# Hybrid encoder trunk, last down projection: token slices of 384 and 128 instead of 256 and 256

## The chip, the cores and the metric

The kernel runs on one core of one Trainium2 chip. The metric is the device time of one execution in microseconds, on the slowest core (here the only one). Three timed runs of the kernel before took 1594.29, 1595.68 and 1596.27 us; the median is 1595.68.

## The reference

Two layers work on 512 tokens of width 1024. Each layer projects a normalized input into three mixers (a retention, a diagonal state-space model, a gated linear attention), merges them with gates, and ends with a squared-ReLU MLP. A final norm follows. What matters here is the last part:

```
    for l in range(DEPTH):                     # DEPTH = 2
        ...
        h2 = rmsnorm(x, norm2_g[l])
        x = x + jnp.square(jax.nn.relu(h2 @ w_ff1[l])) @ w_ff2[l]     # 1024 -> 4096 -> 1024
    return rmsnorm(x, final_norm_g)

def rmsnorm(x, g):
    xf = x.astype(jnp.float32)
    y = xf * lax.rsqrt(jnp.mean(xf * xf, axis=-1, keepdims=True) + EPS)
    return (y * g.astype(jnp.float32)).astype(x.dtype)
```

All of it is float32.

## The kernel before

Everything is kept transposed: features on the 128 partitions, tokens along the free axis. `x` is 8 tiles of 128 features by 512 tokens. A weight chunk of 128 × 1024 (`raw`) is loaded by DMA and split into two fp32r parts, a rounded one (`whi`, line 108, ScalarE) and the rest (`wlo`, line 109, VectorE). Activations are split in the same way (`fh` and `fl` for the hidden tiles of the MLP). A product is then three fp32r matmuls per block of 128 features, high by high, high by low, low by high (lines 125 to 127 in `col_tile`), 24 for one output tile of 128 features, all into one PSUM tile `mm`, of which four rotate.

The MLP's 4096 hidden features are worked through in four quarters. A quarter makes 8 hidden tiles and then multiplies them with the matching part of the second weight matrix, for each of the 8 output tiles `j`, and adds to `x[j]`. For the fourth quarter of the last layer (line 442) the loop is turned: all 8 weight chunks are kept (`ws`), and the tokens are cut into two slices. For each slice the 8 output tiles are computed one after the other (24 matmuls each), each is added to `x` on VectorE (line 451), its square is taken on ScalarE and summed over the tiles on GpSimd (`acc_sq`, lines 174 to 178), and the output times the gain is prepared on ScalarE (`scale_out`, line 241). `emit_out` then ends a slice with the final norm:

- column sums over the features by matmuls of the accumulators with a column of ones, one matmul for each 128 tokens and each of two accumulators (line 155, plain f32);
- the mean and its inverse square root in twelve small VectorE operations on one value per token (lines 158 and 134 to 141);
- a diagonal matrix for each 128 tokens (line 162), and a product with ones (line 164) that spreads the values over all partitions, copied to SBUF by ScalarE (line 166);
- eight products of output and norm, six on VectorE (line 253) and two on GpSimd (line 251), and four DMAs, each for a pair of tiles (line 255).

Each engine works through its own instructions in the order in which a scheduler put them at build time, from dependencies and from the priorities that `hp` sets. The first slice's norm is therefore put between the matmuls of the second slice; the second slice's norm has nothing behind it and ends the kernel.

Of the kernel before, what the change touches and what calls it, by code (L numbers as in the profile page):

```python
# [17 lines left out]
P = 128  # L18
# [21 lines left out]
class Hybrid:  # L40
# [264 lines left out]
    def layer(self, l, h, acc):  # L305
# [69 lines left out]
        for j2 in range(4):  # L375
            w = self.weights(l)
            for i in range(2):
                j = 2 * j2 + i
                ps = self.col_tile(w, yc, base=i * 512)
# [3 lines left out]
        for j4 in range(2):  # L383
            w = self.weights(l)
            for i in range(4):
                j = 4 * j4 + i
                ps = self.col_tile(w, ya, base=i * 256)
# [5 lines left out]
        for j2 in range(4):  # L393
            gb = [gate(8 + 2 * j2 + i) for i in range(2)]
            w = self.weights(l)
            for i in range(2):
                j = 2 * j2 + i
# [12 lines left out]
        for j in range(KT):  # L410
# [4 lines left out]
            ps = self.col_tile(w, ms)  # L415
# [12 lines left out]
        for q in range(4):  # L428
            hid = []
            for f in range(8):  # L430
                w = self.weights(l)
                ps = self.col_tile(w, h2)
                with self.hp(15000):
                    t = self.slot(s="ht")
                    ev = nc.vector.scalar_tensor_tensor(t, ps, 0.0, R2, ALU.max, ALU.mult)  # L435
                    nc.scalar.square(t, t)  # L436
                    hi, lo = self.slot(F32R, s="fh"), self.slot(F32R, s="fl")
                    self.split(hi, lo, t)
                    hid.append((hi, lo))
                if q and f < 6:  # L440
                    self.bg_steps(1, ev)
            if q == 3 and l + 1 == self.depth:
                ws = [self.weights(l, "wt") for _ in range(KT)]
                for sl in (slice(0, 256), slice(256, 512)):
                    acts = [(a[:, sl], b[:, sl]) for a, b in hid]
                    acc, out = [], []
                    for j in range(KT):
                        ps = self.col_tile(ws[j], acts, ps=self.mm([P, 256]))
                        with self.hp(15000):
                            xj = self.x[j][:, sl]  # L450
                            nc.vector.tensor_add(xj, xj, ps)
                            self.acc_sq(acc, xj, j)
                            out.append(self.scale_out(j, sl))
                    with self.hp(15000):
                        self.emit_out(acc, out, sl)
                break
            for j in range(KT):
                w = self.weights(l)
                ps = self.col_tile(w, hid)
                with self.hp(15000):  # L460
                    ev = nc.vector.tensor_add(self.x[j], self.x[j], ps)  # L461
                    if q == 3:
                        xs = self.dr.tile([P, 512], F32, tag=f"xs{j}", bufs=1, name=self.nm("xs"))
                        nc.sync.dma_start(xs, self.x[j])
                        self.xsrc[j] = xs
                        hn.append(self.scaled_split(self.x[j], self.smc(l + 1, SM_G1, j)))
                        self.acc_sq(acc, self.x[j], j, two=False)
                if q < 3 and j < 7:
                    self.bg_steps(2, ev)
# [720 lines left out]
```

## Time and profile before

| | |
|---|---|
| median of three runs | 1595.68 us |
| profiled execution, its own time | 1598.12 us |
| its span, first to last instruction | 1596.2 us |
| TensorE busy in the span | 1567.2 us (98%), 7862 matmul records |
| VectorE, ScalarE, GpSimd busy | 957.3 (60%), 589.4 (37%), 176.1 (11%) us |
| mean granted TensorE clock | 0.988 |
| share of TensorE in the chain that ended last | 87% |

The profiled execution is 2.44 us above the median. Its span leaves out 1.92 us of that execution. PE stands for TensorE's matmuls and PEld for its weight loads, which run beside them; DVE is VectorE, ACT is ScalarE, POOL is GpSimd. A matmul's record is longer than the distance to the next one, since matmuls are pipelined: how often they come is read from starts, not from durations.

### The profile page before, as it was taken

What the parts mean: (1) busy time and instruction counts of PE and PEld (TensorE: products, weight loads), DVE (VectorE), ACT (ScalarE), POOL (GpSimd) and SP (SyncE); (2) the same over time, 40 slices, a digit from 0 to 9 for tenths busy, and PEclk for the clock granted to TensorE, in tenths of its full rate; (3) what the DMA queues carried; (4) which work ended last, traced back from release to release, by engine and by line L of the source; (5) the groups of instructions that cost most, each with busy time, mean ns of one, the idle gap of its engine ahead of it and who ended that gap; (6) DMA issues with size and microseconds to landing.
All of it is one profiled execution on the core that took longest, in us unless ns stands there. A gap on an engine that the chain in (4) does not pass through costs nothing.

```text
span 1596.2 us, 20251 instructions
## 1 busy us (share of the span) xinstructions
PE 1567.2 (98%) x7862; PEld 1320.0 (83%) x7862; DVE 957.3 (60%) x1678; ACT 589.4 (37%) x917; POOL 176.1 (11%) x212
## 2 busy tenths in 40 slices
PE   9998799999999999999999999999999999999997
PEld 6987788888888887888889898878888888888897
DVE  6798888665645747434557858945556534343353
ACT  5543153424434243423425333242334423232242
POOL 0113102331210000000111110210312000000001
PEclk9999799999999999999999999999999999999998
DMA  6522122332432323232335322332334232323221
GB/s 211 167 67 86 60 78 83 107 114 80 150 106 79 107 90 111 80 110 94 128 121 156 93 87 73 106 119 79 102 115 140 93 96 91 105 92 106 92 67 54
DMA packets 60512, 163.35 MB, mean 102 GB/s; under 512 B 10556, under 2 KB 17212, under 8 KB 60416
## 3 DMA queue, kind: packets, MB, share of 16 engines
q1 hardware_dynamic: 60096, 161.01, 31.7%
q8 instruction: 62, 1.02, 0.2%
q0 software_dynamic: 320, 1.05, 0.2%
q14 instruction: 34, 0.28, 0.1%
HBM read 147.11 MB, written 6.52 MB: 96 GB/s over the span
## 4 chain that ended last, share of the span: by engine, by line
PE 87%; DVE 10%; DMA 1%; issue 1%; SPq 0%; POOL 0%; ACT 0%; DVEq 0%; POOLq 0%
PE mm L126 26%; PE mm L127 26%; PE mm L125 26%; DVE wlo L109 1%; PE mm L284 1%; PE mm L286 1%; PE mm L282 1%; PE ms L555 1%; PE ms L1056 1%; DMA rsw<-za 0%; PE ms L1021 0%; DVE mean L642 0%; DMA xp<-xT 0%; PE ms L691 0%; PE ms L155 0%
## 5 line engine op out<-in xcount | busy, mean ns | idle before, releaser
L125 PE MATMUL mm<-hh,whi 128*128 128x512 f32 x1136 | 445.9, 393 | 0.3 <-ACT whi L108 0.3
L127 PE MATMUL mm<-hh,wlo 128*128 128x512 f32 x1136 | 445.4, 393 | 0.6 <-DVE wlo L109 0.6
L126 PE MATMUL mm<-hl,whi 128*128 128x512 f32 x1136 | 445.7, 392 | 0.0
L108 ACT CAST whi<-raw 128x1024 fp32r<-128x1024 f32 (+1 forms) x258 | 266.9, 1043 | 362.4 <-PE mm L127 227.0
L109 DVE TENSOR_TENSOR wlo<-raw,whi 128x1024 fp32r<-128x1024 f32 (+1 forms) x258 | 341.6, 1325 | 87.5 <-PE mm L126 65.6
L125 PEld LDWEIGHTS mm<-hh,whi 128*128 128x128 f32 x1136 | 214.2, 189 | 45.4 <-issue 1.2
L127 PEld LDWEIGHTS mm<-hh,wlo 128*128 128x128 f32 x1136 | 214.0, 188 | 44.8 <-DVE wlo L109 1.3
L126 PEld LDWEIGHTS mm<-hl,whi 128*128 128x128 f32 x1136 | 214.1, 188 | 44.7 <-issue 0.7
L126 PE MATMUL mm<-fl,whi 128*128 128x512 f32 (+1 forms) x576 | 210.9, 366 | 0.0
L127 PE MATMUL mm<-fh,wlo 128*128 128x512 f32 (+1 forms) x576 | 210.5, 366 | 0.0
L125 PE MATMUL mm<-fh,whi 128*128 128x512 f32 (+1 forms) x576 | 209.5, 366 | 0.0
L126 PEld LDWEIGHTS mm<-fl,whi 128*128 128x128 f32 x576 | 108.6, 189 | 17.7
L125 PEld LDWEIGHTS mm<-fh,whi 128*128 128x128 f32 x576 | 108.5, 189 | 17.6
L127 PEld LDWEIGHTS mm<-fh,wlo 128*128 128x128 f32 x576 | 108.6, 189 | 17.5
L178 POOL TENSOR_TENSOR acc<-acc,sq 128x512 f32<-128x512 f32 (+1 forms) x30 | 33.7, 1123 | 683.0 <-ACT sq L177 680.5
L461 DVE TENSOR_TENSOR x<-x,mm 128x512 f32<-128x512 f32 x56 | 38.4, 685 | 113.8 <-PE mm L127 113.8
L436 ACT ACTIVATE ht<-ht 128x512 f32<-128x512 f32 x64 | 40.4, 632 | 152.2 <-DVE ht L435 152.2
L435 DVE SCALAR_TENSOR_TENSOR ht<-mm,R 128x512 f32<-128x512 f32 x64 | 44.1, 689 | 86.4 <-PE mm L127 75.1
L114 DVE TENSOR_TENSOR fl<-ht,fh 128x512 fp32r<-128x512 f32 x64 | 44.2, 691 | 69.1 <-ACT fh L113 69.0
L369 ACT ACTIVATE g<-g,cst 128x512 f32<-128x512 f32 x48 | 34.8, 724 | 114.0 <-DVE g L368 113.8
L126 PE MATMUL mm<-y,whi 128*128 128x512 f32 x160 | 62.2, 389 | 0.0
L127 PE MATMUL mm<-y,wlo 128*128 128x512 f32 x160 | 62.2, 389 | 0.0
(266 smaller groups left out, 2049.6 us busy)
## 6 DMA issues: line engine op xcount, KB each, us to landing
raw<-wst SPq DMA_DIRECT2D x254, 512.0 KB, 3.7
dup<-zc SPq DMA_DIRECT2D x32, 128.0 KB, 3.6
rsw<-za SPq DMA_DIRECT2D x32, 64.0 KB, 2.6
qfb<-za SPq DMA_DIRECT2D x16, 128.0 KB, 4.2
x<-xT SPq DMA_DIRECT2D x8, 256.0 KB, 4.0
xs<-x SPq DMA_DIRECT2D x8, 256.0 KB, 2.9
x<-xs SPq DMA_DIRECT2D x8, 256.0 KB, 4.4
outT<-out SPq DMA_DIRECT2D x8, 256.0 KB, 2.7
```

The source lines that it names most:

```text
L108: nc.scalar.copy(hi[:, s], raw[:, s])
L109: nc.vector.tensor_sub(lo[:, s], raw[:, s], hi[:, s].bitcast(F32))
L114: self.nc.vector.tensor_sub(lo, src, hi.bitcast(F32))
L125: nc.tensor.matmul(ps, hi[:, o:o + P], a, start=first and k == 0, stop=False)
L126: nc.tensor.matmul(ps, hi[:, o:o + P], b, start=False, stop=False)
L127: nc.tensor.matmul(ps, lo[:, o:o + P], a, start=False, stop=last and k == n - 1)
L178: return (eng or (nc.vector if j == KT - 1 else nc.gpsimd)).tensor_add(accs[0], accs[0], t)
L282: nc.tensor.matmul(o, a[:, s], hi[:, k * 256:(k + 1) * 256], start=f, stop=False, skip_group_check=True)
L369: nc.scalar.activation(g, g, AF.Sigmoid, bias=self.smc(l, SM_BM, j))
L435: ev = nc.vector.scalar_tensor_tensor(t, ps, 0.0, R2, ALU.max, ALU.mult)
L436: nc.scalar.square(t, t)
L461: ev = nc.vector.tensor_add(self.x[j], self.x[j], ps)
```

## The change

The two slices of tokens have 384 and 128 tokens instead of 256 and 256, and the PSUM tile takes its width from the slice.

```diff
             if q == 3 and l + 1 == self.depth:
                 ws = [self.weights(l, "wt") for _ in range(KT)]
-                for sl in (slice(0, 256), slice(256, 512)):
+                for sl in (slice(0, 384), slice(384, 512)):
                     acts = [(a[:, sl], b[:, sl]) for a, b in hid]
                     acc, out = [], []
                     for j in range(KT):
-                        ps = self.col_tile(ws[j], acts, ps=self.mm([P, 256]))
+                        ps = self.col_tile(ws[j], acts, ps=self.mm([P, sl.stop - sl.start]))
```

Both kernels have the same number of instructions on each engine. Of column sums and diagonal products the first slice now has three for each accumulator or norm and the second one, instead of two and two.

On TensorE, in the first output tile of the second slice, before (`mm_12543` is its PSUM tile, `acc_12287` an accumulator of the first slice, the last column the output's shape):

```order
L125 MATMUL mm_12543<-fh_12057,whi_12215 128x256
L126 MATMUL mm_12543<-fl_12058,whi_12215 128x256
L127 MATMUL mm_12543<-fh_12057,wlo_12216 128x256
L155 MATMUL ms_12503<-cst,acc_12287 128x1 x2
L125 MATMUL mm_12543<-fh_12095,whi_12215 128x256
L126 MATMUL mm_12543<-fl_12096,whi_12215 128x256
```

The same place after the change, where that tile is `mm_12546`:

```order
L125 MATMUL mm_12546<-fh_12019,whi_12215 128x128
L126 MATMUL mm_12546<-fl_12020,whi_12215 128x128
L127 MATMUL mm_12546<-fh_12019,wlo_12216 128x128
L155 MATMUL ms_12503<-cst,acc_12287 128x1 x3
L125 MATMUL mm_12546<-fh_12057,whi_12215 128x128
L126 MATMUL mm_12546<-fl_12058,whi_12215 128x128
```

The second slice's matmuls have 128 columns, and the first slice's column sums, now three, stand three matmuls earlier in it.

On VectorE, in the middle of the second slice, before (line 451 adds a tile of the second slice, lines 141 and 162 belong to the first slice's norm, line 253 multiplies the first slice's outputs by it):

```order
L141 SCALAR_TENSOR_TENSOR ny_12512<-nu_12514,ny_12512 128x2
L451 TENSOR_TENSOR x_9918<-x_9918,mm_12573 128x256
L162 TENSOR_SCALAR dg_12524<-cst,ny_12512 128x128 x2
L451 TENSOR_TENSOR x_9959<-x_9959,mm_12603 128x256
L253 TENSOR_TENSOR out_12289<-out_12289,ms_12527 128x256 x2
L253 TENSOR_TENSOR out_12350<-out_12350,ms_12527 128x256
L253 TENSOR_TENSOR out_12411<-out_12411,ms_12527 128x256 x2
L253 TENSOR_TENSOR out_12472<-out_12472,ms_12527 128x256
L451 TENSOR_TENSOR x_10000<-x_10000,mm_12634 128x256
```

The same place after the change:

```order
L140 TENSOR_TENSOR nu_12516<-nu_12516,nv_12510 128x3
L451 TENSOR_TENSOR x_9918<-x_9918,mm_12576 128x128
L141 SCALAR_TENSOR_TENSOR ny_12514<-nu_12516,ny_12514 128x3
L162 TENSOR_SCALAR dg_12526<-cst,ny_12514 128x128 x3
L451 TENSOR_TENSOR x_9959<-x_9959,mm_12606 128x128
L253 TENSOR_TENSOR out_12289<-out_12289,ms_12530 128x384 x2
L253 TENSOR_TENSOR out_12350<-out_12350,ms_12530 128x384
L253 TENSOR_TENSOR out_12411<-out_12411,ms_12530 128x384 x2
L253 TENSOR_TENSOR out_12472<-out_12472,ms_12530 128x384
L451 TENSOR_TENSOR x_10000<-x_10000,mm_12637 128x128
```

The second slice's second addition stands one place earlier, there are three diagonal products, and the first slice's products with the norm are 384 columns wide, still ahead of the fourth addition.

## Rows read from the trace of the kernel before

**Rows 1.** Busy time by stretch: us, PE, PEld, DVE, ACT, POOL, clock, DMA.

```profile
1536.60:1560.77 24.17, 24.17 (x202) 24.13 (x202) 5.79 (x11) 7.65 (x18) 4.43 (x6) 1.00 0.00 1
1560.77:1583.85 23.08, 23.08 (x195) 23.02 (x193) 7.28 (x27) 6.14 (x16) 5.82 (x8) 1.00 0.14 47
1583.85:1596.20 12.35, 2.15 (x9) 1.27 (x9) 4.93 (x21) 1.19 (x3) 1.41 (x2) 0.67 0.25 85
```

**Rows 2.** Timeline, VectorE: start, us, line, names, shapes, idle before and releaser.

```profile
1503.84 0.69 DVE L435 SCALAR_TENSOR_TENSOR ht<-mm,R 128x512 f32<-128x512 f32 x1 [1.57 <-PE mm L127]
1509.28 0.69 DVE L435 SCALAR_TENSOR_TENSOR ht<-mm,R 128x512 f32<-128x512 f32 x1 [1.57 <-PE mm L127]
...
1553.78 0.42 DVE L451 TENSOR_TENSOR x<-x,mm 128x256 f32<-128x256 f32 x1 [2.46 <-PE mm L127]
1556.65 0.42 DVE L451 TENSOR_TENSOR x<-x,mm 128x256 f32<-128x256 f32 x1 [2.46 <-PE mm L127]
```

**Rows 3.** Timeline, TensorE: f32 passes of 128 and of 64 moving columns.

```profile
263.25 1.95 PE L1021 MATMUL ms<-U,s5PT 128*128 128x128 f32 x16
264.95 0.48 PE L127 MATMUL mm<-hh,wlo 128*128 128x512 f32 x1
265.27 0.40 PE L125 MATMUL mm<-hh,whi 128*128 128x512 f32 x1
...
962.35 0.39 PE L691 MATMUL ms<-v,rsT 128*128 128x64 f32 x2
962.57 0.39 PE L692 MATMUL ms<-rS,qfb 128*128 128x64 f32 x2
```

**Rows 4.** Weight loads by shape: line, names, shapes, count, busy us, mean ns.

```profile
L125 PEld LDWEIGHTS mm<-fh,whi 128*128 128x128 f32 x576 | 108.5, 189 | 17.6
...
L1021 PEld LDWEIGHTS ms<-U,s5PT 128*128 128x128 f32 x128 | 15.8, 192 | 0.5
```

**Rows 5.** Chain that ended last, in time order: start, us, what.

```profile
1583.88 0.43 DVE x L451
1584.33 0.42 ACT acc L174
...
1584.80 0.62 PE ms L155 x4
...
1587.81 0.49 DVE dg L162 x2
...
1588.35 1.23 PE ms L164 x2
...
1589.60 0.38 ACT R L166
...
1590.01 0.42 DVE out L253
...
1590.76 1.32 DVE out L253 x4
```

**Rows 6.** Groups by shape: count, busy us, mean ns, idle before and releaser.

```profile
L461 DVE TENSOR_TENSOR x<-x,mm 128x512 f32<-128x512 f32 x56 | 38.4, 685 | 113.8 <-PE mm L127 113.8
...
L177 ACT ACTIVATE sq<-x 128x512 f32<-128x512 f32 x21 | 12.9, 616 | 0.0
...
L451 DVE TENSOR_TENSOR x<-x,mm 128x256 f32<-128x256 f32 x16 | 6.6, 420 | 32.4 <-PE mm L127 32.4
...
L177 ACT ACTIVATE sq<-x 128x256 f32<-128x256 f32 x12 | 5.0, 416 | 21.4 <-DVE x L451 21.4
```

**Rows 7.** Page, DMA issues: name, queue, count, KB each, us to landing.

```profile
raw<-wst SPq DMA_DIRECT2D x254, 512.0 KB, 3.7
...
outT<-out SPq DMA_DIRECT2D x8, 256.0 KB, 2.7
```

**Rows 8.** Busy time by stretch again: columns as in the first group.

```profile
1588.00:1589.00 1.00, 0.66 (x2) 0.50 (x2) 0.29 (x2) 0.00 (x0) 0.00 (x0) 0.54 0.00 0
1012.00:1015.00 3.00, 3.00 (x14) 2.46 (x14) 2.11 (x2) 0.00 (x0) 2.20 (x4) 1.00 0.00 0
```

## Prediction

> **What bounds the kernel now.** I read the busy shares by stretch first, then the distance between matmuls in the timeline, then the chain of waits of the end. In the stretch of the first token slice and in that of the second, TensorE is busy from end to end (24.17 of 24.17 us and 23.08 of 23.08), while VectorE, ScalarE and GpSimd each work less than a third of the time [rows 1]. So the two slices cost what their matmuls cost, and nothing on another engine matters there unless it becomes very late. After 1583.85 us of the span comes a tail of 12.35 us in which TensorE works 2.15 us: the chain of waits there is one operation after another, each waiting for the one before [rows 5]. The change touches both: the matmuls of the slices, and the width of the tail's operations.
>
> **The matmuls of the two slices.** Each slice has 8 output tiles of 8 × 3 = 24 matmuls, so 192 matmuls, whatever its width. Their spacing is read between additions that each wait for the last matmul of a tile of 24. Tiles of 512 tokens end at 1503.84 and 1509.28: 5.44 us / 24 = 0.227 us a matmul. Tiles of 256 end at 1553.78 and 1556.65: 2.87 / 24 = 0.120 us [rows 2]. (192 × 0.120 = 23.0 us, which is the second stretch of [rows 1].) A matmul with 384 columns lies between these two and I take the middle, 0.173 us. First slice: 192 × (0.173 − 0.120) = +10.2 us.
>
> The straight line through the same two points would give 0.067 us for 128 columns, and then the second slice would give back exactly those 10.2 us. That is the question of this change, because no row shows an fp32r matmul with fewer than 256 columns. Every matmul of these slices has its own weight load of 128 columns before it. The nearest rows are the plain f32 matmuls, which the chip runs as two passes (the 64 matmuls that line 1021 issues show as 128 rows [rows 4]), each with its own load of 128 columns. Sixteen such passes of 128 moving columns and one 512-column matmul fill 263.25 to 265.27 us: 2.02 − 0.227 = 1.79 us, or 0.112 us a pass. Two passes of only 64 moving columns start 0.22 us before the next two: 0.111 us a pass [rows 3]. Half the moving columns buy nothing, so it is the load that sets the pace there, at 0.11 us. And the load records are alike: 189 ns for the fp32r weights of this very product, 192 ns for the f32 weights [rows 4]. I conclude that a 128-column fp32r matmul comes every 0.112 us, hardly sooner than a 256-column one. Second slice: 192 × (0.112 − 0.120) = −1.5 us. Bounds: 0.067 us (the line, no load in the way) and 0.224 us (an fp32r matmul that is as dear as a whole f32 one, two passes of 0.112). Inside my own reading the spacing could also stay at 0.120 us, if the 0.008 us between the f32 pass and the 256-column fp32r matmul belong to the fp32r load.
>
> The Trainium skill, "TensorE: Matmul & The Clock Gate", section "LDWEIGHTS (loading the stationary operand)", speaks against this change: a load's time goes by its weight columns alone, columns divided by 1.2 in ns, which for 128 is 107 ns; the f32 passes above agree (111 to 112 ns with 64 and with 128 moving columns), and by 107 ns the second slice's term would be −2.5 us instead of −1.5.
>
> **What stands between them.** The norm of the first slice is computed inside the second slice's stream. It takes three column sums per accumulator instead of two, with two accumulators and two passes each: 4 more passes of 0.112 = +0.4 us, and its broadcast product has 128 more columns in two passes, +0.2 us. Together +0.6 us on TensorE. On VectorE the six products with the broadcast norm (line 253) get wider, 384 columns, and stand ahead of the second slice's fourth addition: by 1.03 ns a column [rows 6] they take some 0.13 us more each, 0.8 us in all. A tile of 24 matmuls lasts 2.7 us and four PSUM tiles rotate, so TensorE does not wait; were that cover gone, the price would be those 0.8 us. The first slice's wider outputs leave during the second slice, where the transfer engines are busy 14% of the time [rows 1]; they cost nothing.
>
> **The tail.** Its operations have 128 columns instead of 256. Per column VectorE takes (685 − 420) / 256 = 1.03 ns and ScalarE (616 − 416) / 256 = 0.78 ns [rows 6]. Against the chain [rows 5]: addition −0.13; square −0.10; the last column sum, two passes fewer of 0.11, −0.2 (the other accumulator's sum runs beside the addition); the twelve small operations between sum and diagonal, now on one value a partition instead of two, unchanged; one diagonal product fewer, −0.2; the broadcast product, two passes of 128 columns less. That one runs at half the granted clock (0.54 in its microsecond [rows 8]), so 2 × 0.22 = −0.45; the copy of the norm −0.10; six products with the norm 6 × 0.13 = −0.8. The output transfers carry half the bytes, but their 2.7 us from issue to landing [rows 7] are mostly not bytes: 512 KB take 3.7, so 128 KB less would be some −0.5, of which I take −0.3, since four transfers overlap. Sum: −2.3 us. Between −1.6 (no gain from transfers, little from the half-clock product) and −3.0.
>
> **The sum**: +10.2 − 1.5 + 0.6 − 2.3 = +7.0 us. The profiled execution took 1598.12 us for a span of 1596.2, so it would go to 1605.1. It is itself 2.4 us above the median of the runs, 1595.68, and I carry the difference over to the median: **1602.7 us**, slower by 0.44%. With 0.120 us in the second slice it is +8.5; with 0.111 and a tail gain of 3.0, +6.1; and the spacings are read to some 0.003 us, 192 times which is 0.6 us either way. So 1600.5 to 1605.0 is the likeliest case's own range.
>
> **Rivals.** *First, not slower: the load of fp32r weights gets out of the way.* If the second slice's loads took 0.067 us or less, the two slices together would cost what they did, and the tail decides: 0 + 0.6 − 2.3 = −1.7, 1594.0 us, no measurable change. It turns at a spacing of 0.076 us (7.0 us / 192 below my 0.112). For it: at 256 columns the spacing of 0.120 us is still above that of the f32 passes, so no fp32r row shows a load in the way. Against it: the equal load records, and the passes of 64 columns that did not get faster. Chance 0.12. The Trainium skill, "TensorE: Matmul & The Clock Gate", section "Back-to-back issue gap", has about 81 ns for sustained load-and-matmul pairs of 128 columns; the f32 passes of this trace disagree (111 to 112), and by 81 ns the sum would be an estimated +1.0 us, 1596.7, no change either.
>
> *Second, much slower: a narrow fp32r matmul is as dear as an f32 one.* Then the second slice's spacing is 0.224 us: 192 × (0.224 − 0.120) = +20.0 instead of −1.5, in all +28.5 us, 1624.2. For it: all fp32r products of the kernel have 256 columns or more, so the trace says nothing of narrower ones; f32 passes of 128 columns exist, and are that dear for a whole product. Against it: from 512 to 256 columns nothing of the kind begins, and nothing in the rows says why it should. Chance 0.17.
>
> *Third, the clock falls.* In the second slice the array would stream columns about half of the time (0.053 us by the slope of [rows 2], out of 0.112). If the granted clock fell to its lower level, loads would take twice as long: up to 192 × 0.112 = +21.5 more, 1624, or less if it falls late. Against it: the clock stays at 1.00 from 1012 to 1015 us, where only 14 matmuls ran [rows 8], and in the tail it fell after TensorE had nothing to do between the column sum, over at 1585.42, and the product at 1588.35 [rows 5, 8]. Chance 0.05.
>
> **The numbers.** My reading has 0.66, the quick load 0.12, the dear narrow matmul 0.17, the clock 0.05. The range 1599 to 1625 holds my reading and both dear cases, and leaves out the quick load and a small rest of my own. A difference of 0.2% (3.2 us) is about what a measurement of this kernel can tell from none, so no change means 1592.5 to 1598.9: most of the quick-load case and a sliver of mine, where load and tail both come out well, 0.11. Faster: the quick-load case with a tail that gains all its bound, 0.04. Slower: 0.85.
>
> **What would show it.** In the changed kernel's timeline the additions of the first slice should stand 24 × 0.173 = 4.16 us apart, those of the second 24 × 0.112 = 2.7 us (1.6 for the quick load, 5.4 for the two dear cases; the granted clock of the stretch tells these two apart). The stretch of the first slice should be some 10 us longer, that of the second about 1 us shorter, and the tail some 2.3 us shorter, with the norm's small operations as long as before. The weight loads of the second slice should follow each other without a gap. I am wrong if the second slice takes less than some 18 us or more than 25.

## The result, and the profile after

The changed kernel took 1602.66 us (median of 20 executions) against 1595.45 for the kernel before (20 executions): ratio of the means 1.0081 with a 95% interval of 1.0058 to 1.0104, over all executions but the last one named here. It is slower, and 1602.7 was forecast. But 19 of the 20 executions fall into two groups: twelve from 1600.64 to 1604.29 us (median 1602.05, mean granted clock 0.988 to 0.990), seven from 1617.92 to 1622.43 (median 1619.03, mean clock 0.976 to 0.979); the twentieth, 5602.59 us, is far off for a reason that no profile shows. The kernel before has one group, 1594.05 to 1597.93. That the overall median stands at 1602.66 is luck of the draw: with a few more of the long ones it would be 1618. The profile described here is of the first group (1601.77 us, span 1599.9).

Three stretches, cut at the additions (line 451) that end each slice: from the last hidden tile's operation to the end of the first slice, the second slice, the tail. First the kernel before (columns as in [rows 1]: the first number after the stretch is its length), cut anew, since the cut of [rows 1] lay 1.2 us inside the second slice:

```profile
1536.86:1559.54 22.68, 22.68 (x191) 22.68 (x190) 5.38 (x11) 6.87 (x16) 4.43 (x6) 1.00 0.00 1
1559.54:1583.88 24.34, 24.34 (x205) 24.29 (x203) 7.70 (x29) 6.92 (x17) 5.82 (x8) 1.00 0.13 45
1583.88:1596.20 12.32, 2.12 (x9) 1.24 (x8) 4.92 (x21) 1.19 (x3) 1.41 (x2) 0.67 0.25 85
```

The same three stretches after the change:

```profile
1533.99:1566.78 32.79, 32.79 (x192) 32.79 (x190) 6.39 (x11) 8.38 (x16) 6.08 (x6) 1.00 0.00 1
1566.78:1590.15 23.37, 23.37 (x208) 23.11 (x206) 8.09 (x29) 5.72 (x17) 4.75 (x8) 1.00 0.19 69
1590.15:1599.90 9.75, 1.31 (x6) 0.84 (x5) 3.75 (x20) 0.86 (x3) 0.87 (x2) 0.62 0.19 54
```

The first stretch grew from 22.68 to 32.79 us (+10.1), the second shrank from 24.34 to 23.37 (−1.0), the tail from 12.32 to 9.75 (−2.6). Together +6.6 us, which is also the distance of the first group's median from the kernel before (1602.05 − 1595.45, ratio 1.0041). TensorE is busy throughout both slices, as in [rows 1], and its clock is at 1.00.

The additions in the timeline of VectorE after the change answer to [rows 2]:

```profile
1554.30 0.56 DVE L451 TENSOR_TENSOR x<-x,mm 128x384 f32<-128x384 f32 x1 [3.60 <-PE mm L127]
1558.46 0.55 DVE L451 TENSOR_TENSOR x<-x,mm 128x384 f32<-128x384 f32 x1 [3.60 <-PE mm L127]
...
1584.80 0.29 DVE L451 TENSOR_TENSOR x<-x,mm 128x128 f32<-128x128 f32 x1 [2.40 <-PE mm L127]
1587.47 0.29 DVE L451 TENSOR_TENSOR x<-x,mm 128x128 f32<-128x128 f32 x1 [2.39 <-PE mm L127]
```

Tiles of the first slice end 4.16 us apart, 24 matmuls of 0.173; tiles of the second end 2.67 us apart, 24 of 0.111. Half the columns of before, and 7% less time. The groups by shape are these (first the weight loads, all shapes of this product together, then the matmuls of the second slice; count, busy us, mean ns):

```profile
L125 PEld LDWEIGHTS mm<-fh,whi 128*128 128x128 f32 x576 | 108.4, 188 | 17.6
...
L125 PE MATMUL mm<-fh,whi 128*128 128x128 f32 x64 | 17.6, 275 | 0.0
```

The loads are what they were in [rows 4], 188 ns in the mean, and hardly depend on how many columns follow: ahead of 384 columns their records last 188 ns, in the stretch of 128 columns 192. That they set the distance is what the experiments below test.

The chain that ended last, for [rows 5]:

```profile
1590.15 0.30 DVE x L451
1590.47 0.32 ACT acc L174
...
1590.84 0.40 PE ms L155 x2
...
1593.57 0.30 DVE dg L162
1593.91 0.81 PE ms L164 x2
1594.74 0.27 ACT R L166
1595.04 0.29 DVE out L253
...
1595.53 0.79 DVE out L253 x4
```

Every width-dependent step became shorter and the twelve small operations did not: from the start of the first of them to the diagonal 2.31 us (1591.26 to 1593.57), before 2.37 (1585.44 to 1587.81). The output transfer, against [rows 7]:

```profile
outT<-out SPq DMA_DIRECT2D x4, 128.0 KB, 1.9
```

From issue to landing 1.9 us instead of 2.7, at half the bytes.

### The profile page after: what moved, and what is told of

It is laid out like the page before. It is cut to its first block, busy times and chain, and to the rows that moved or that the text cites. A ratio compares the mean times of both kernels' runs of the same rounds, so it can differ in the third digit from the quotient of the medians.

```text
span 1599.9 us, 20246 instructions
## 1 busy us (share of the span) xinstructions
PE 1572.8 (98%) x7862; PEld 1326.3 (83%) x7862; DVE 956.2 (60%) x1678; ACT 589.0 (37%) x917; POOL 176.2 (11%) x212
## 4 chain that ended last, share of the span: by engine, by line
PE 89%; DVE 8%; DMA 1%; issue 1%; SPq 0%; POOL 0%; ACT 0%; DVEq 0%; POOLq 0%
PE mm L126 26%; PE mm L125 26%; PE mm L127 26%; DVE wlo L109 1%; PE mm L284 1%; PE mm L286 1%; PE mm L282 1%; PE ms L555 1%; PE ms L1056 1%; PE ms L1021 0%; DMA rsw<-za 0%; DVE mean L642 0%; DMA xp<-xT 0%; PE ms L670 0%; PE ms L155 0%
## 5 line engine op out<-in xcount | busy, mean ns | idle before, releaser
L126 PE MATMUL mm<-fl,whi 128*128 128x512 f32 (+2 forms) x576 | 213.7, 371 | 0.0
L127 PE MATMUL mm<-fh,wlo 128*128 128x512 f32 (+2 forms) x576 | 213.3, 371 | 0.0
L125 PE MATMUL mm<-fh,whi 128*128 128x512 f32 (+2 forms) x576 | 212.5, 371 | 0.0
L125 PEld LDWEIGHTS mm<-fh,whi 128*128 128x128 f32 x576 | 108.4, 188 | 17.6
L126 PEld LDWEIGHTS mm<-fl,whi 128*128 128x128 f32 x576 | 108.4, 188 | 17.6
L178 POOL TENSOR_TENSOR acc<-acc,sq 128x512 f32<-128x512 f32 (+2 forms) x30 | 33.7, 1122 | 690.6 <-ACT sq L177 690.6
```

The lines of the kernel that those rows point to most:

```text
L125: nc.tensor.matmul(ps, hi[:, o:o + P], a, start=first and k == 0, stop=False)
L126: nc.tensor.matmul(ps, hi[:, o:o + P], b, start=False, stop=False)
L127: nc.tensor.matmul(ps, lo[:, o:o + P], a, start=False, stop=last and k == n - 1)
L178: return (eng or (nc.vector if j == KT - 1 else nc.gpsimd)).tensor_add(accs[0], accs[0], t)
```

## The experiments

The theory: a weight load of 128 columns is a floor under the distance of matmuls, 0.112 us, whatever streams through them. The first rival: narrow matmuls cost what they cost for another reason. The second question, which the result put, was where the long executions come from.

**The changed kernel again** (no edit).

> The changed kernel once more, unaltered. Its 20 executions fell into two groups: 13 from 1600.6 to 1604.3 us with a mean granted TensorE clock of 0.988 to 0.990, seven from 1617.9 to 1622.4 us with 0.976 to 0.979 (one more execution was far off). Theory A (my third rival come true in part of the executions): in the long ones the granted clock falls to its lower level while the 128-column slice runs, and each of some 150 of its 192 matmuls takes 0.223 us instead of 0.112, +16.7 us. Then again about a third of the executions lie 16 to 20 us above the rest, each with a mean clock lower by some 0.011; a profile of such a one would show 0.50 in the second slice and matmuls 0.22 us apart, and nothing else longer. Theory B: the long executions come from elsewhere (a late weight transfer, a disturbance of the whole core): then they need not carry the lower clock, and their extra time lies outside the second slice.

Six executions: 1601.72 and 1603.31; 1618.25, 1618.32, 1619.27 and 1619.45, these with a mean clock of 0.978 to 0.979. (The count of the first group above is twelve, not 13 as the expectation has it.) The profiled one is long. Its additions of the end of the first slice and of the last three tiles of the second:

```profile
1566.12 0.56 DVE L451 TENSOR_TENSOR x<-x,mm 128x384 f32<-128x384 f32 x1 [3.60 <-PE mm L127]
...
1596.18 0.29 DVE L451 TENSOR_TENSOR x<-x,mm 128x128 f32<-128x128 f32 x1 [4.83 <-PE mm L127]
1601.30 0.29 DVE L451 TENSOR_TENSOR x<-x,mm 128x128 f32<-128x128 f32 x1 [4.83 <-PE mm L127]
1606.42 0.29 DVE L451 TENSOR_TENSOR x<-x,mm 128x128 f32<-128x128 f32 x1 [4.83 <-PE mm L127]
```

The tiles are 5.12 us apart, 0.213 us a matmul, and the second slice takes 40.30 us (1566.12 to 1606.42) instead of 23.37, +16.9. Nothing else grew by as much as half a microsecond. Its clock, by the microsecond (busy TensorE, weight loads and so on; the third number from the end is the granted clock):

```profile
1569.00:1570.00 1.00, 1.00 (x12) 1.00 (x11) 0.29 (x1) 0.26 (x1) 0.00 (x0) 1.00 0.00 0
1570.00:1571.00 1.00, 1.00 (x10) 1.00 (x10) 0.71 (x5) 0.05 (x1) 0.00 (x0) 0.89 0.00 0
1571.00:1572.00 1.00, 1.00 (x6) 1.00 (x6) 0.83 (x6) 0.00 (x0) 0.00 (x0) 0.50 0.06 16
```

And its matmuls at that place:

```profile
1569.33 0.78 PE L155 MATMUL ms<-cst,acc 128*128 128x1 f32 x6
1569.97 0.31 PE L126 MATMUL mm<-fl,whi 128*128 128x128 f32 x1
...
1570.68 0.30 PE L126 MATMUL mm<-fl,whi 128*128 128x128 f32 x1
1570.79 0.40 PE L127 MATMUL mm<-fh,wlo 128*128 128x128 f32 x1
1570.99 0.41 PE L125 MATMUL mm<-fh,whi 128*128 128x128 f32 x1
1571.20 0.41 PE L126 MATMUL mm<-fl,whi 128*128 128x128 f32 x1
```

The clock goes from full to half at about 1570.9 us, 5 us into the slice, while TensorE has work in every moment: the matmuls' distance steps from 0.11 to 0.21 us and stays there until the end. Theory B falls; theory A has the place and the price. What stands just ahead of the fall are two groups of six column-sum passes (at 1566.88 and 1569.33), of one moving column each. The same two groups stand at the same place of the slice in the profile of the first group, where the clock stayed.

**Half the weight columns in the second slice.**

```diff
-ps = self.col_tile(ws[j], acts, ps=self.mm([P, sl.stop - sl.start]))
+m = 64 if sl.start else P; ps = self.col_tile(ws[j], acts, ps=self.mm([P, sl.stop - sl.start])[0:m], m=m)
```

with `o + m` for `o + P` in the three matmuls and the addition on the first `m` partitions.

> In the 128-column slice each matmul uses only the first 64 columns of its weights, so the load before it is half as wide and the number of moving columns stays 128. The upper 64 features of each output tile are left out in this slice. If the weight load sets the pace (my step): the load takes half, some 0.056 us, and the moving columns become the limit at the line's 0.067 us; the second slice gives back 192 x 0.045 = 8.6 us, in all some 1594 us (against 1602.2 for the changed kernel), with the clock staying at 1.00 since the array streams without gaps. If a matmul of few moving columns has a price of its own, whatever its load: spacing stays at 0.112 us and the time at about 1602.

1592.92 us (ten executions, 1589.92 to 1593.86), ratio to the kernel before 0.9983 (0.9974 to 0.9991). Two additions of the second slice, and its weight loads:

```profile
1573.19 0.28 DVE L451 TENSOR_TENSOR x<-x,mm 64x128 f32<-64x128 f32 x1
1574.63 0.28 DVE L451 TENSOR_TENSOR x<-x,mm 64x128 f32<-64x128 f32 x1
```

```profile
L125 PEld LDWEIGHTS mm<-fh,whi 128*64 128x64 f32 x64 | 8.7, 135 | 0.2 <-issue 0.2
```

Loads of 64 columns record 135 ns instead of 188, and a tile takes 1.44 us: 0.060 us a matmul with the same 128 moving columns that took 0.111. A price of narrow matmuls as such is excluded: the floor goes by the weight columns. With half the weight columns a matmul also makes half as many outputs, and no run parts these two; that it is the load is read from its records, which are shorter too. The 0.060 us is even less than the line's 0.067.

**256 columns through the array, 128 used.**

```diff
-acts = [(a[:, sl], b[:, sl]) for a, b in hid]
+wide = slice(256, 512) if sl.start else sl; acts = [(a[:, wide], b[:, wide]) for a, b in hid]
...
-ps = self.col_tile(ws[j], acts, ps=self.mm([P, sl.stop - sl.start]))
+ps = self.col_tile(ws[j], acts, ps=self.mm([P, wide.stop - wide.start]))[:, sl.start - wide.start:]
```

> The changed kernel, but in the second slice each matmul streams 256 columns (tokens 256 to 511) of which only the last 128 are used, so that width of additions, norm and tail stay those of the change. Load theory: spacing 0.120 us instead of 0.112, 192 x 0.008 = +1.5 us, some 1603.7 us. Theory A of the two groups (the clock falls because the 128-column slice leaves the array unused about half of the time): no execution near 1619, all within 3 us. Theory B (long executions come from elsewhere): a third of them again 16 to 20 us longer.

1603.21 us, five executions from 1603.12 to 1605.89, none long; ratio 1.0052 (1.0040 to 1.0064). The second slice's additions:

```profile
1588.67 0.29 DVE L451 TENSOR_TENSOR x<-x,mm 128x128 f32<-128x128 f32 x1 [2.59 <-PE mm L127]
1591.55 0.29 DVE L451 TENSOR_TENSOR x<-x,mm 128x128 f32<-128x128 f32 x1 [2.59 <-PE mm L127]
```

2.88 us a tile, 0.120 us a matmul: doubling the moving columns costs 0.21 us a tile. And with 256 columns in each matmul the clock stayed, in these five executions, although the one-column sums stand in this stream too.

**64 columns at a time in the second slice** (the 24 matmuls of a tile are made twice, for 64 tokens each; the one line of the edit is written out here as a loop).

```diff
+for c in range(0, sl.stop - sl.start, w):    # w = 64 in the second slice
+    self.col_tile(ws[j], [(x[:, c:c + w], y[:, c:c + w]) for x, y in acts], ps=ps[:, c:c + w])
```

> The changed kernel, but the second slice's products are made in two halves of 64 columns: 384 matmuls of 64 columns instead of 192 of 128, each with its own load of 128 weight columns; all other operations as in the change. Load theory: every matmul still takes 0.111 us at the full clock, so the second slice takes 42.6 us instead of 21.5: +21 us, some 1623 us in an execution whose clock stays up. With the array streaming only a quarter of the time, theory A lets the clock fall in most or all executions: then up to another +43 us, 1666. If a narrow matmul's price went by its columns: spacing 0.056 us, about 1602.

1660.81 us (four executions, 1660.31 to 1662.38), all with a mean clock of 0.965 to 0.966; ratio 1.0410 (1.0395 to 1.0426). Two matmuls while the clock was still up, and two additions later:

```profile
1568.11 0.28 PE L127 MATMUL mm<-fh,wlo 128*128 128x64 f32 x1
1568.22 0.28 PE L125 MATMUL mm<-fh,whi 128*128 128x64 f32 x1
```

```profile
1628.19 0.29 DVE L451 TENSOR_TENSOR x<-x,mm 128x128 f32<-128x128 f32 x1 [9.95 <-PE mm L127]
1638.43 0.29 DVE L451 TENSOR_TENSOR x<-x,mm 128x128 f32<-128x128 f32 x1 [9.95 <-PE mm L127]
```

0.11 us a matmul at the full clock and 10.24 / 48 = 0.213 us at the lower one, the same as for 128 columns in both. Here the clock fell every time. In the profiled execution it fell in the second of these stretches, at about 1573.6 us, 1.6 us after the second group of one-column sums had ended:

```profile
1571.00:1573.00 2.00, 2.00 (x20) 2.00 (x20) 0.67 (x5) 0.00 (x0) 0.00 (x0) 1.00 0.00 0
1573.00:1575.00 2.00, 2.00 (x14) 2.00 (x14) 1.72 (x11) 0.00 (x0) 0.00 (x0) 0.65 0.04 8
```

**The narrow slice first.** `(slice(0, 128), slice(128, 512))`.

> The changed slices in the other order, 128 tokens first and 384 last. Matmuls as in the change (192 at 0.112 us, 192 at 0.173). My terms, against the changed kernel's 1602 us: the norm between the slices is now that of 128 tokens, 8 column-sum passes of 0.112 and two passes of 0.213 in the broadcast product fewer, -1.3; the tail is that of 384 tokens, 256 columns wider, twice my tail term, +4.6; together some 1605.5 us in executions whose clock stays up. Theory A of the clock (it falls because of the 128-column stream, wherever that stands): part of the executions again longer by up to 16 us, with the lower clock in the first slice. Theory C (it falls only because the narrow slice stands last, after everything else has run out): no long executions.

1605.28 us (four executions, 1604.07 to 1607.02), ratio 1.0065 (1.0050 to 1.0080), 0.2 from the sum. The narrow slice from the end of its third tile on, and the tail:

```profile
1541.82:1555.22 13.40, 13.40 (x121) 13.40 (x121) 1.44 (x5) 3.01 (x10) 2.29 (x5) 1.00 0.00 1
1589.27:1604.20 14.93, 3.01 (x13) 1.69 (x12) 6.06 (x22) 1.51 (x3) 1.96 (x2) 0.61 0.29 105
```

The clock is at 1.00 through these 13 us of the 128-column stream, and the tail of 384 tokens takes 14.93 us. No execution was long, but four are too few to say that none is (0.52 to the fourth, by the share of all executions below, is 0.07). What differs from the change, beside the place, is that no column sums stand in the narrow stream: they come after it.

**One slice.** `(slice(0, 512),)`.

> One slice of 512 tokens: the slicing taken away. Matmuls: 192 x 0.227 = 43.5 us instead of 2 x 23.0 in the kernel before, -2.5; no norm between slices, 8 passes of 0.112 and two of 0.213 fewer, -1.3; the tail 256 columns wider than before, twice my tail term, +4.6: +0.8 us, 1595.7 against 1594.9, no measurable change. If wider matmuls are worth more than I think, or the tail's width less, it beats both kernels.

1597.06 us (ten executions), ratio 1.0013 (1.0004 to 1.0022): no better than the kernel before, which took 1595.23 us beside it, +1.8 where the sum had +0.8. In its profile the stretch from the last hidden tile to the end is 60.4 us against 59.3 before, +1.1; the tail was dearer than my term had it, 17.6 us against 12.32, +5.3 instead of +4.6. The tails of 128, 256, 384 and 512 tokens last 9.75, 12.32, 14.93 and 17.6 us: 2.6 us for each 128 tokens, where I had 2.3.

**192 columns at a time in the first slice** (the loop of the 64-column kernel, with `w = 192` in the first slice).

> The changed kernel, but the first slice's products are made in two halves of 192 columns, 384 matmuls instead of 192 of 384 columns. If the weight load is a floor under the spacing (0.112 us for 128 weight columns): 384 x 0.112 = 42.9 us instead of 33.3, +9.6, some 1611.5 us where the clock stays up. If the line through the wider matmuls held here (192 columns: 0.093 us) and only narrow ones leave it: 384 x 0.093 = 35.8, +2.5, some 1604.5.

1612.19 us (four executions, 1611.54 to 1614.84), ratio 1.0112 (1.0095 to 1.0129). Two additions of the first slice:

```profile
1560.93 0.55 DVE L451 TENSOR_TENSOR x<-x,mm 128x384 f32<-128x384 f32 x1 [4.81 <-PE mm L127]
1566.29 0.55 DVE L451 TENSOR_TENSOR x<-x,mm 128x384 f32<-128x384 f32 x1 [4.81 <-PE mm L127]
```

5.36 us / 48 = 0.112 us, not 0.093: the floor holds at 192 columns too. None of the four executions was long (clock 0.987 to 0.989). Here too a 128-column stream follows, with the second group of one-column sums in it (at 1580.91 us of the profile); the first group (1576.03) still stands in the 192-column stream. Four are again too few to say that this is the reason.

**Wide column sums.** The first slice's sums, inside the narrow stream, with 128 moving columns instead of one.

```diff
-ps = self.ms([P, nt])
+c = P if nt == 3 else 1; ps = self.ms([P, nt * c])
...
-nc.tensor.matmul(ps[:, i:i + 1], a[:, i * P:(i + 1) * P], self.ones[:, 0:1], start=n == 0 and i == 0,
+nc.tensor.matmul(ps[:, i * c:(i + 1) * c], a[:, i * P:(i + 1) * P], self.ones[:, 0:c], start=n == 0 and i == 0,
...
-nc.vector.tensor_scalar(v, ps, 1.0 / D, EPS, ALU.mult, ALU.add)
+nc.vector.tensor_scalar(v, ps[:, ::c], 1.0 / D, EPS, ALU.mult, ALU.add)
```

> The changed kernel, but the first slice's column sums, which stand inside the 128-column stream (12 passes of 0.112 us with a single moving column, in two groups of six), multiply with all 128 columns of ones instead of one; the norm reads every 128th column of the result. The load sets their spacing, so the passes should keep 0.112 us and the long executions aside the time should be the changed kernel's, 1602 us. Theory D: in the long execution that was profiled the clock fell 0.9 us after the second group of sums; it is these sums, in which the array takes in one column where it could take 128, together with the narrow stream that tip the clock. Then no execution near 1618. Theory A alone (the narrow stream is enough, the sums' place by the fall is chance): about 4 in 10 executions stay at 1618 to 1622.

1601.21 us, five executions from 1600.78 to 1603.89, none long; ratio 1.0039 (1.0026 to 1.0053).

```profile
1569.43 0.88 PE L155 MATMUL ms<-cst,acc 128*128 128x128 f32 x6
1570.07 0.31 PE L126 MATMUL mm<-fl,whi 128*128 128x128 f32 x1
```

```profile
1566.00:1570.00 4.00, 4.00 (x38) 4.00 (x37) 0.84 (x2) 1.19 (x3) 0.00 (x0) 1.00 0.00 0
1570.00:1574.00 4.00, 4.00 (x38) 4.00 (x38) 2.89 (x16) 0.46 (x2) 0.42 (x1) 1.00 0.01 4
```

Six passes still take 0.64 us until the next matmul, as with one column (1569.33 to 1569.97 above): the load hides the other 127. The clock stays at 1.00 where it fell before.

**The control on the same chip** (no edit).

> The changed kernel unaltered on the same chip, as the control of the run above: 11 of 25 executions so far were 16 to 20 us longer, so about 4 in 10 here, each with a mean clock of about 0.978 instead of 0.989.

Four of six executions long (1618.57 to 1621.58, clock 0.976 to 0.978), two at 1600.97 and 1601.68.

**Wide column sums again.**

> The kernel with the wide column sums once more, since five executions without a long one could be chance (0.55 to the fifth is 0.05 if the sums don't matter). Theory D: none of these near 1618 either, all at 1600.5 to 1604.5. Theory A alone: about 4 in 10 at 1618 to 1622.

1601.93 us, five executions from 1601.17 to 1603.43; ratio 1.0039 (1.0025 to 1.0053). This was another chip than in the first five executions, and the changed kernel was not run beside it. Of the changed kernel 15 in 31 executions were long, leaving out the one far off; with wide sums 0 in 10. At a share of 15 in 31 chance alone would give that once in some 750 tries, and once in some 210 if the share itself is only known from these 41 executions. This bears theory D out: the 128-column stream with both groups of one-column sums in it lost the clock in about half of the executions, the same stream with full sums in none. No version that makes all outputs beat the kernel before.

## Why the prediction was right, and where it was not

- *The first slice's matmuls*: +10.2 forecast, +10.1 measured. The middle between 0.227 and 0.120 was the spacing of 384 columns.
- *The second slice*: −1.5 for the matmuls and +0.6 for the norm inside it, −0.9; measured −1.0. The step that decided the sign, taking the f32 passes' 0.112 us for fp32r because the load records were alike, was right, and the half-wide load shows that it was right for its reason: the floor goes by the weight columns.
- *The tail*: −2.3 forecast, −2.6 measured. Addition 0.43 to 0.30, square 0.42 to 0.32, sum 0.62 to 0.40, diagonal 0.49 to 0.30, broadcast 1.23 to 0.81, copy 0.38 to 0.27, products 2.07 to 1.28 us are within 0.03 of their terms; from the last product to the end of the span 4.12 to 3.58, −0.54 where I took −0.3. The output transfers, which I had worked out at −0.5 and taken at −0.3, landed 0.8 us sooner in the median (1.9 against 2.7); the −0.5 was nearer.
- *The sum* of the three stretches is +6.6 where the prediction had +7.0. That the overall median lies within 0.1 us of the forecast is luck; the first group's median, 1602.05, is the figure that the sum can be held to.
- *The side remark* that set 192 × 0.120 beside the second stretch of [rows 1] fitted by accident: that stretch began inside the slice, and the slice with its norm took 24.34 us. The term rested on the additions and was not touched by it.
- *The first rival*, a load out of the way, fell with the spacing of 0.111 us; the *second*, a narrow fp32r matmul as dear as an f32 one, with it and with the 0.060 us of the half-wide load.
- *The third rival*, the clock, was mis-sized. I gave it 0.05 and it happened in 15 of 31 executions. Its price was right in kind: 0.213 us a matmul, from about 1570.9 us on, +16.9 us of an upper bound of 21.5. What I weighed against it, a stretch from 1012 to 1015 us at 1.00 with few matmuls [rows 8], said nothing of a stream that is narrow for 20 us and has column sums in it. The other argument, that the clock fell in the tail after TensorE had had nothing to do, made a pause the condition; in the long execution it fell without one. So the forecast holds for the executions whose clock stays, about half, and for the rest the time is 1619, inside the range but not in the likeliest case's own.

Two things stay open. Why the same instructions keep the clock in one execution and lose it in another: in the second slice of the two traces I found no difference ahead of the fall but the place in time (the second group of sums at 1569.99 us of the span in the one, 1569.33 in the other), and the control's profile, with that group at 1569.18 us, kept the clock, so the place does not sort them either. And whether the 128-column stream alone could tip it: in 14 executions without one-column sums in it (ten with wide sums, four with the narrow slice first) it did not.

## What to carry to other kernels

Before a matmul is made narrower, compare its moving columns with its weight load: here a load of 128 fp32r columns takes 0.112 us, so that 192, 128 and 64 moving columns cost the same, and nothing under an estimated 240 gets cheaper (where the line through 0.120 us for 256 and 0.227 for 512 meets 0.112). An uneven cut then pays for the wide part without a rebate on the narrow one. In such a stream small things can also cost the full clock: here it fell to half in 15 of 31 executions with one-column sums in the 128-column stream, and in none of ten with 128-column sums. So look at the granted clock of more than one execution before trusting a median. Where the load hides them, moving columns are free (0.64 us for six sums of one column and of 128), and filling them was the cure here.

## What was not expected of the hardware

- The granted clock fell from 1.00 to 0.50 while TensorE had work without a gap, and not in every execution; the fall that [rows 8] shows came after TensorE had stood idle.
- At the lower clock 64 and 128 moving columns both take 0.213 us, nearly twice the 0.111: the load slows down with the clock. Its records do so too, 333 ns in the mean of the long execution's second slice after the fall, against 192.
- The fixed part of the spacing was smaller with the narrower load. With 128 weight columns the line through 512 and 256 moving columns leaves 0.013 us beside the columns (0.120 − 0.107, where 0.107 is the difference of the two spacings), and 384 columns lie on it (0.173 − 0.160); with 64 weight columns 128 moving columns, the one width measured, leave 0.060 − 0.053 = 0.007.
- A sum over partitions with one moving column costs the same as with 128: 0.64 us for six passes and the way to the next matmul in both.
